# Gate and decay arithmetic of a gated-linear-attention layer, spread in 21 steps over the projections of keys, queries and values

## The chip, the cores and the metric

The kernel runs on one core of a Trainium2 chip. A core has a tensor engine for matrix products (PE, with its weight loads shown as PEld), a vector engine (DVE), a scalar engine for functions such as Exp (ACT), a general engine (POOL) and a queue engine that issues most transfers (SP). Each engine works through its own list of instructions in order and waits at an instruction until what it needs is there. The metric is the device time of one execution in microseconds (us); three runs before the change gave 1467.38 us in the median (1467.37 to 1469.64).

## The reference

One layer of a streaming encoder: a token mixer of two kinds of heads, cross-attention to 256 memory tokens, and an MLP, all on 1024 tokens of width 1024. What the change touches is the start of the mixer:

```python
proj = xn @ w_in                       # xn = rms_norm(x)
fq, fk, fv, ff, gq, gk, gv, glr, gr = split(proj)
fq = rms_norm(fq per head); fk = rms_norm(fk per head)
log_f = log_sigmoid(ff + fox_b_f)                       # 8 forget gates a token
g_log = log_sigmoid(glr @ gla_w_gate2 + gla_b_gate) / 16  # 256 decays a token
# gated linear attention, chunks of 64 tokens:
bc = cumsum(g_log over the chunk)
q_dec = gq * 64**-0.5 * exp(bc);  k_dec = gk * exp(-bc)
A = tril(q_dec @ k_dec.T);  o = A @ gv + q_dec @ state
```

The forgetting attention (called fox in the code) uses the cumulated sum of log_f as a bias on its scores.

## The kernel before, in words

All products are made of float32 operands split into two parts (hi and lo), so one tile of 128 tokens by 512 columns takes 3 x 8 matmuls of 512 columns (`gemm`, L108 to L110). The weights of 512 columns come in four transfers (`raw`, two buffers, L78); ACT makes the hi part `wh` (L97) and DVE the lo part `wl` (L98). The pool of `wh` and `wl` has nine places each, so the weights of the next projection can only be made as the last tile of the present one lets go of its own.

`mixer_inputs` runs, in this order of the program: the GLA queries and keys (`gqk`), the small columns for gates (`smallz`), the gate arithmetic, eight tiles of fox keys (`normed`, into `kd`), eight tiles of fox queries (`normed`, into `qd`), eight tiles of GLA values (`gv`, L492), then the GLA loop over eight blocks (L509 on, which begins with `ga`, L519), and the fox values (`evac_split` into `vd`).

A tile of keys or queries in `normed` goes: 24 matmuls into a PSUM bank (four banks), ACT squares it (`sq`, L141), DVE sums the squares (`ss`, L143), POOL makes the reciprocal root (`rs_v`, `rs_r`, L126 and L127), DVE scales the tile (`sq`, L304), for queries POOL multiplies by a gain (L306), PE transposes it (`tr`, L309, two PSUM banks), ACT and DVE split it (`qn`, L115 and L116), and SP writes it out.

The gate arithmetic has three rows of work: the forget gates (8 partitions, `small`, `fu`, `lf`) and two tiles of decays (128 partitions by 1024, `z` from PE at L432, then `ls`, `kdec` and `qdec` as scratch). For each: DVE min, ACT Abs and Exp, DVE add (L437 to L440), two more DVE operations (L441, L442), ACT Ln and DVE subtract (L444, L445). Then `forget` (a scan over the tokens, a split, eight small writes to `cq` and `ck`), two scans over the decays (L454), the chunk ends `La` and `Lb`, `dec`, and at L471 to L477 four Exp of the whole tile, which make `qdec` (DVE, L475) and `kdec` (POOL, L477). The first matmul that needs these two is `ga` at L519.

The order of instructions on each engine is set by a scheduler from the program's order and its own estimate of times. In the program the gate arithmetic stands wholly ahead of the keys, and L471 to L477 ahead of the queries. Behind the mixer's inputs come the fox stage (softmax blocks, with "side work" between them: half of the output projection and the keys and values of the memory, through a tile `mkv` with one buffer, written to `kTd` and `vmd`), the rest of the output projection, the cross-attention and the MLP.

Of the kernel before, what the change touches and what calls it, by code (L numbers as in the profile page):

```python
# [17 lines left out]
F32 = mybir.dt.float32  # L18
# [3 lines left out]
AF = mybir.ActivationFunctionType  # L22
ALU = mybir.AluOpType
AX = mybir.AxisListType
PSUM = bass.MemoryType.PSUM
# [5 lines left out]
P = 128  # L31
KT = D // P
NT = S // P
# [5 lines left out]
C_MIX, C_XAT, C_MEM, C_MLP, C_BG, C_FB = 0, 8, 16, 24, 32, 34  # L39
# [5 lines left out]
W_FQ, W_FK, W_FV, W_FF, W_GQ, W_GK, W_GV, W_GLR, W_GR = 0, 512, 1024, 1536, 1544, 1800, 2056, 2568, 2584  # L45


def f(ap):
    return ap.bitcast(F32)


class Layer:
# [59 lines left out]
    def evac_split(self, hi, lo, ps, scale=None):  # L112
        nc = self.nc
        if scale is None:
            nc.scalar.activation(hi, ps, AF.Copy)  # L115
            nc.vector.tensor_tensor(lo, ps, f(hi), ALU.subtract)  # L116
        else:
            nc.scalar.activation(hi, ps, AF.Identity, scale=scale)
            nc.vector.scalar_tensor_tensor(lo, ps, scale, f(hi), ALU.mult, ALU.subtract)

    def rstd(self, out, ss, inv_n, eps=EPS):

# [146 lines left out]
    def mixer_inputs(self):  # L269
        nc = self.nc  # L270
        w_in = self.w_in
        with ExitStack() as st:
# [24 lines left out]

            def normed(t, W, dst, g=None):

                ps = token_major(t, W)  # L300
                v3 = lambda ap: ap.rearrange("p (h d) -> p h d", h=8)
                qn = self.T(stp, [P, 512], F32, "sq")
                r = self.head_rstd(ps, qn, 8, self.xev[:, t:t + 1])
                nc.vector.tensor_tensor(v3(qn), v3(ps), self.bcast(r, 64), ALU.mult)  # L304
                if g is not None:
                    nc.gpsimd.tensor_tensor(v3(qn), v3(qn), g.unsqueeze(1).to_broadcast([P, 8, 64]), ALU.mult)  # L306
                tp = self.T(trp, [P, 512], F32, "tr")
                for j in range(4):
                    nc.tensor.transpose(tp[:, j * P:(j + 1) * P], qn[:, j * P:(j + 1) * P], self.ident)  # L309
                q2 = self.T(stp, [P, 2, 4, P], F32R, "qn")  # L310
                self.evac_split(q2[:, 0], q2[:, 1], tp.rearrange("p (a b) -> p a b", a=4))
                for a in range(2):
                    for i in range(2):
                        nc.sync.dma_start(dst[a::2, i, :, t * P:(t + 1) * P].rearrange("h d s -> d h s"),
                                          f(q2[64 * a:64 * a + 64, i]))

            gqk = self.mixg.rearrange("p t k s -> p (t k s)").rearrange("p (i s) -> p i s", i=4)
            with ExitStack() as s2:  # L320
# [14 lines left out]
                def factors(t):  # L335
# [23 lines left out]
                for i in range(4):  # L359
                    ps = next(gbanks)  # L360
# [3 lines left out]
                with self.tc.issue_after(x_load.ins):  # L364
                    W = self.wsplit(w_in[:, W_FK:W_FK + 512], C_MIX)
# [13 lines left out]
            for k in range(KT):  # L379
                g = self.cols[:, C_MIX + k:C_MIX + k + 1]  # L380
# [18 lines left out]
            g3 = self.T(gp, [96, 256], F32R, "g3")  # L399
# [10 lines left out]
            qdec = self.T(decp, [P, 2, 2, S], F32, "qdec")  # L410
            kdec = self.T(decp, [P, 2, S], F32, "kdec")
# [12 lines left out]

            R = slice(32, 40)
            gates = [(small[R], self.cols[R, C_FB:C_FB + 1], small[R], f(fu[R]), lf[R])]
            for ft in range(2):
                z = self.T(zps, [P, 2, 512], F32, "z")  # L430
                for h in range(2):
                    nc.tensor.matmul(z[:, h, :], g3[:, ft * P:(ft + 1) * P], s3[:, h * 512:(h + 1) * 512],  # L432
                                     start=True, stop=True)
                gates.append((z.rearrange("p a b -> p (a b)"), self.cols[:, C_BG + ft:C_BG + ft + 1], kdec[:, ft, :],
                              qdec[:, 0, ft, :], ls[:, ft, :]))
            for z, b, e, u, out in gates:
                nc.vector.tensor_scalar(out, z, b, 0.0, ALU.add, ALU.min)  # L437
                nc.scalar.activation(e, z, AF.Abs, bias=b)
                nc.scalar.activation(e, e, AF.Exp, scale=-1.0)
                nc.vector.tensor_scalar(u, e, 1.0, None, ALU.add)  # L440
                nc.vector.scalar_tensor_tensor(e, u, -1.0, e, ALU.add, ALU.subtract)  # L441
                nc.vector.tensor_tensor(out, out, e, ALU.add)  # L442
            for z, b, e, u, out in gates:
                nc.scalar.activation(u, u, AF.Ln)  # L444
                nc.vector.tensor_tensor(out, out, u, ALU.subtract)  # L445
            self.forget(lf, fu, ones)

            nc.gpsimd.memset(qdec[64:128, :, 0, :], 0.0)
            nc.gpsimd.memset(qdec[0:64, :, 1, :], 0.0)


            for ft in range(2):
                bc = kdec[:, ft, :]
                nc.vector.tensor_tensor_scan(bc, seg, ls[:, ft, :], 0.0, ALU.mult, ALU.add)  # L454
                v = bc.rearrange("p (c s) -> p c s", s=P)
                nc.vector.tensor_copy(La[:, ft, :].unsqueeze(2), v[:, :, 63:64])
                nc.vector.tensor_copy(Lb[:, ft, :].unsqueeze(2), v[:, :, 127:128])
                nc.vector.tensor_tensor(v[:, :, 0:64], v[:, :, 0:64], self.bcast(La[:, ft, :], 64), ALU.subtract)
            nc.vector.tensor_tensor(dec[:, :, 0:7], Lb[:, :, 0:7], La[:, :, 1:8], ALU.add)
            nc.scalar.activation(dec[:, :, 0:7], dec[:, :, 0:7], AF.Exp, scale=1.0 / 16)  # L460


            for t in range(NT):
                normed(t, W, self.kd)

            W = self.wsplit(w_in[:, W_FQ:W_FQ + 512], C_MIX)

            for i in range(4):
                ft = i % 2
                e = ls[:, ft, :]  # L470
                nc.scalar.activation(e, kdec[:, ft, :], AF.Exp, scale=(1.0 if i < 2 else -1.0) / 16)  # L471
                if i < 2:
                    for a in range(2):
                        r = slice(64 * a, 64 * a + 64)
                        nc.vector.scalar_tensor_tensor(qdec[r, ft, a, :], gqk[r, i, :], 0.125, e[r], ALU.mult, ALU.mult)  # L475
                else:
                    nc.gpsimd.tensor_tensor(kdec[:, ft, :], gqk[:, i, :], e, ALU.mult)  # L477

            for t in range(NT):
                normed(t, W, self.qd, self.gfox)  # L480
            gst.close()
            banks = self.two(mmp, 1, mmp, 1)

            gps = self.open(glst, "gps", 1, space=PSUM)

# [3 lines left out]
            W = self.wsplit(w_in[:, W_GV:W_GV + 512], C_MIX)  # L489
            for t in range(NT):  # L490
                ps = token_major(t, W)
                nc.scalar.activation(gv[:, t, :], ps, AF.Identity, scale=self.xr2[:, t:t + 1])  # L492


            glp = self.open(glst, "gl", 2)
# [77 lines left out]
    def forget(self, lf, ch, ones):  # L573

        nc = self.nc
        R, R0 = slice(32, 40), slice(0, 8)
        nc.gpsimd.memset(ones[R], 1.0)
        nc.vector.tensor_tensor_scan(lf[R], ones[R], lf[R], 0.0, ALU.mult, ALU.add)
        nc.scalar.activation(ch[R], lf[R], AF.Copy)
        nc.vector.tensor_tensor(lf[R], lf[R], f(ch[R]), ALU.subtract)  # L580
        nc.sync.dma_start(self.cq[:, 0, :], ones[R])
# [8 lines left out]
        nc.sync.dma_start(self.ck[:, 1, :], lf[R0])  # L590


    def fox_open(self):
# [721 lines left out]
```

## Time and profile before

| what | value |
|---|---|
| median of three runs | 1467.38 us |
| the profiled execution | 1473.37 us |
| its span from first to last instruction | 1471.6 us |
| PE busy | 1435.6 us (98%) |
| DVE, ACT, POOL busy | 934.8, 685.1, 431.7 us |
| granted PE clock, mean | 0.989 |

The profiled execution is 5.99 us longer than the median of the runs without a profile, and 1.8 us of it lie outside the span. A "waits" view lists, for one engine, the idle time in front of a line and the instruction that ended it. A "timeline" gives start, duration and instruction in order of time; the start of a matmul and its end overlap with its neighbours, so the time that one costs is read as the distance between starts. A "windows" view gives the busy time of each engine in a stretch, with the granted PE clock (1.00 is full speed).

### The profile page before, as it was taken

The page shows a single profiled execution, that of the slowest core. Times are in us where ns is not written, and L with a number is a line of the kernel's source. Part 1 is how long each engine was busy: PE and PEld are TensorE (multiplying, and loading weights), DVE is VectorE, ACT ScalarE, POOL GpSimd, SP SyncE. Part 2 cuts the span into 40 slices and gives each one's busy share as a digit, 9 for nine tenths or more (in the row PEclk, how much of TensorE's full clock was granted, in tenths as well). Part 3 has the DMA queues.
Part 4 walks back from the last instruction along what each step waited for, and adds up shares of the span by engine and source line. Part 5 has one row for each costly group of instructions (what it writes and reads, how often), then busy time and mean ns, then how long its engine had stood idle before and what let it go on. Part 6 is the DMA issues. An engine that isn't in the chain of part 4 may idle for free.

```text
span 1471.6 us, 19266 instructions
## 1 busy us (share of the span) xinstructions
PE 1435.6 (98%) x7068; PEld 1198.2 (81%) x7068; DVE 934.8 (64%) x1328; ACT 685.1 (47%) x1095; POOL 431.7 (29%) x456
## 2 busy tenths in 40 slices
PE   9999999999998999999999999999999999999998
PEld 7777888887877787888888878887888878888887
DVE  5387412427776676656654885645556958788797
ACT  4464322326776555445442254545445736334230
POOL 4146503324473311621212200000000532333454
PEclk9999999999999999999999999999999999999999
DMA  7425620268576742414375124444445846337353
GB/s 273 124 47 129 153 74 4 72 159 266 181 205 197 194 156 70 144 38 136 115 243 214 44 72 172 172 172 162 169 160 212 313 132 210 126 110 231 108 205 122
DMA packets 121166, 223.94 MB, mean 152 GB/s; under 512 B 8912, under 2 KB 54512, under 8 KB 118512
## 3 DMA queue, kind: packets, MB, share of 16 engines
q1 hardware_dynamic: 119776, 218.25, 45.9%
q10 hardware_dynamic: 1296, 4.46, 1.0%
q8 instruction: 56, 0.92, 0.3%
q14 instruction: 38, 0.31, 0.1%
HBM read 150.59 MB, written 72.09 MB: 151 GB/s over the span
## 4 chain that ended last, share of the span: by engine, by line
PE 82%; DMA 7%; DVE 4%; ACT 3%; issue 2%; POOL 1%; SPq 0%; DVEq 0%; ACTq 0%
PE mm L108 14%; PE mm L109 14%; PE mm L110 13%; PE my L109 7%; PE my L110 7%; PE my L108 7%; PE tr L109 3%; PE tr L108 3%; PE tr L110 3%; PE tr L668 2%; DMA xt<-in_x_dram 1%; DMA raw<-in_w_in_dram 1%; PE pv L675 1%; PE pv L676 1%; PE s L628 1%
## 5 line engine op out<-in xcount | busy, mean ns | idle before, releaser
L108 PE MATMUL my<-x,g 128*128 128x512 f32 x464 | 180.8, 390 | 1.5 <-ACT h L1251 1.5
L109 PE MATMUL my<-x,g 128*128 128x512 f32 x464 | 180.9, 390 | 1.3 <-DVE x L1046 1.3
L110 PE MATMUL my<-x,g 128*128 128x512 f32 x464 | 180.7, 390 | 0.0
L108 PE MATMUL mm<-wh,xh 128*128 128x512 f32 x320 | 128.7, 403 | 0.3 <-ACT wh L97 0.3
L109 PE MATMUL mm<-wl,xh 128*128 128x512 f32 x320 | 127.7, 399 | 0.0
L110 PE MATMUL mm<-wh,xl 128*128 128x512 f32 x320 | 127.4, 398 | 0.0
L1045 ACT ACTIVATE g<-s 128x1024 fp32r<-128x1024 f32 (+1 forms) x72 | 68.9, 963 | 103.9 <-PE my L110 37.6
L1046 DVE TENSOR_TENSOR g<-raw,g 128x512 fp32r<-128x512 f32 (+3 forms) x72 | 67.9, 946 | 69.2 <-ACT g L1045 69.1
L1071 POOL TENSOR_TENSOR s<-raw 128x384 f32<-128x384 f32 (+1 forms) x20 | 25.6, 1279 | 282.9 <-issue 217.0
L108 PEld LDWEIGHTS my<-x,g 128*128 128x128 f32 x464 | 87.2, 188 | 19.9 <-ACT h L1251 1.9
L109 PEld LDWEIGHTS my<-x,g 128*128 128x128 f32 x464 | 87.2, 188 | 19.6 <-DVE x L1046 1.7
L1045 ACT ACTIVATE g<-raw 128x512 fp32r<-128x512 f32 (+3 forms) x72 | 55.5, 773 | 101.8 <-DMA raw<-in_mlp_w_dram 39.9
L110 PEld LDWEIGHTS my<-x,g 128*128 128x128 f32 x464 | 87.2, 188 | 18.0
L1046 DVE TENSOR_TENSOR g<-s,g 128x1024 fp32r<-128x1024 f32 (+1 forms) x72 | 88.7, 1236 | 7.2 <-ACT g L1045 7.2
L639 POOL TENSOR_SCALAR p<-p,rrec 128x128 f32<-128x128 f32 (+3 forms) x64 | 50.6, 792 | 126.6 <-DVE rrec L638 117.0
L1213 DVE TENSOR_TENSOR x<-x 128x1024 fp32r<-128x1024 f32 (+1 forms) x64 | 77.1, 1226 | 15.7 <-ACT x L1212 15.7
L108 PE MATMUL mm<-x,g 128*128 128x512 f32 x220 | 85.9, 390 | 0.0
L110 PE MATMUL mm<-x,g 128*128 128x512 f32 x220 | 85.8, 390 | 0.0
L109 PE MATMUL mm<-x,g 128*128 128x512 f32 x220 | 85.7, 390 | 0.0
L108 PE MATMUL tr<-x,g 128*128 128x512 f32 x212 | 82.6, 389 | 0.0
L110 PE MATMUL tr<-x,g 128*128 128x512 f32 x212 | 82.6, 389 | 0.0
L109 PE MATMUL tr<-x,g 128*128 128x512 f32 x212 | 82.6, 389 | 0.0
(319 smaller groups left out, 3787.3 us busy)
## 6 DMA issues: line engine op xcount, KB each, us to landing
ud<-h SPq DMA_DIRECT2D x32, 768.0 KB
x<-ud SPq DMA_DIRECT2D x48, 512.0 KB
raw<-in_mlp_w_dram SPq DMA_DIRECT2D x20, 1024.0 KB
raw<-in_mlp_w_dram SPq DMA_DIRECT2D x16, 768.0 KB
raw<-in_w_in_dram SPq DMA_DIRECT2D x23, 512.0 KB
raw<-in_xattn_wkv_dram SPq DMA_DIRECT2D x16, 512.0 KB
od<-o SPq DMA_DIRECT2D x32, 256.0 KB
ud<-h SPq DMA_DIRECT2D x32, 256.0 KB
```

The costliest lines, as they stand in the source:

```text
L108: mm(ps, lh[k], rh[k], start=start and k == 0, stop=False, **kw)
L109: mm(ps, lh[k], rl[k], start=False, stop=False, **kw)
L110: mm(ps, ll[k], rh[k], start=False, stop=stop and k == n - 1, **kw)
L628: nc.tensor.matmul(ps[:, c], qa[:, ts], ka[:, c], start=True, stop=False)
L639: nc.gpsimd.tensor_scalar(p[:, 0:n], p[:, 0:n], rr, 1.0, ALU.mult, ALU.mult)
L668: nc.tensor.transpose(o, pp[i][:, kb * P:(kb + 1) * P], self.ident)
L675: nc.tensor.matmul(pv, va[:, kb, :], th[:, js], start=kb == 0, stop=False)
L676: nc.tensor.matmul(pv, va[:, kb, :], tl[:, js], start=False, stop=kb == nb - 1)
L1045: self.nc.scalar.activation(hi, src, AF.Copy)
L1046: self.nc.vector.tensor_tensor(lo, src, f(hi), ALU.subtract)
L1071: eng.tensor_tensor(s[:, 0], raw[:, 3], raw[:, 2], ALU.add)
L1213: nc.vector.tensor_tensor(lo, f(lo), f(hi), ALU.subtract)
```

## The change

The gate and decay arithmetic becomes a generator, `decays()`, that stops at 21 places. The function `step(*ends)` runs it to the next stop and puts everything it makes on an engine behind the instruction of that engine that is given in `ends`. A step is taken behind the eviction (`evac_split`: one instruction of ACT and one of DVE) of key tiles 0 to 5, of query tiles 0 to 5, and behind the ACT eviction of each of the eight tiles of `gv`; there only the ACT instructions of the step are tied, and POOL's are tied nowhere. What is left runs after the last `gv` tile. The two tiles of decays now go ahead of the forget gates; all three Abs and Exp come before the three Ln; the forget gates' scan and their writes come behind the Ln; and the PSUM pools of `z` and of the fourth bank are held until the end of the `gv` tiles. No arithmetic is added or left out.

```diff
     def evac_split(self, hi, lo, ps, scale=None):
...
+            a = nc.scalar.activation(hi, ps, AF.Copy)
+            v = nc.vector.tensor_tensor(lo, ps, f(hi), ALU.subtract)
...
+        return a.ins, v.ins
...
+            def decays():
+                gates = []
+                for ft in (0, 1, None):
...
                     nc.vector.tensor_scalar(out, z, b, 0.0, ALU.add, ALU.min)
                     nc.scalar.activation(e, z, AF.Abs, bias=b)
                     nc.scalar.activation(e, e, AF.Exp, scale=-1.0)
                     nc.vector.tensor_scalar(u, e, 1.0, None, ALU.add)
+                    yield
                     nc.vector.scalar_tensor_tensor(e, u, -1.0, e, ALU.add, ALU.subtract)
                     nc.vector.tensor_tensor(out, out, e, ALU.add)
+                    gates.append((u, out))
+                    yield
+                for u, out in gates:
+                    nc.scalar.activation(u, u, AF.Ln)
+                    nc.vector.tensor_tensor(out, out, u, ALU.subtract)
+                    yield
+                yield from self.forget(lf, fu, ones)
...
+            beside = decays()
+
+            def step(*ends):
+                with ExitStack() as behind:
+                    for ins in ends:
+                        behind.enter_context(self.tc.issue_after(ins))
+                    next(beside, None)
+
+            for cols, dst, g in ((W_FK, self.kd, None), (W_FQ, self.qd, self.gfox)):
+                if cols == W_FQ:
+                    W = self.wsplit(w_in[:, cols:cols + 512], C_MIX)
+                for t in range(NT):
+                    ends = normed(t, W, dst, g)
+                    if t < 6:
+                        step(*ends)
...
             for t in range(NT):
                 ps = token_major(t, W)
-                nc.scalar.activation(gv[:, t, :], ps, AF.Identity, scale=self.xr2[:, t:t + 1])
+                step(nc.scalar.activation(gv[:, t, :], ps, AF.Identity, scale=self.xr2[:, t:t + 1]).ins)
+            for _ in beside:
+                pass
+            gst.close()
```

The order that results on the engines differs at these places. The numbers behind the names tell tiles apart; they are not the same in both kernels.

On DVE, in the middle of the key tiles, before the change (`kdec`, `qdec`, `ls`, `La`, `Lb` are the decays; `sq`, `ss`, `qn` belong to the key tiles):

```order
L116 TENSOR_TENSOR qn_863<-tr_858,qn_863 128x512
L143 TENSOR_REDUCE ss_183_943<-sq_941 128x8
L454 SCALAR_TENSOR_TENSOR kdec_664<-seg_655,ls_675 128x1024
L304 TENSOR_TENSOR sq_895<-mm_870,rs_r_899 128x512
L441 SCALAR_TENSOR_TENSOR kdec_664<-qdec_663,kdec_664 128x1024
L456 COPY La_669<-kdec_664 128x8
L457 COPY Lb_670<-kdec_664 128x8
L304 TENSOR_TENSOR sq_941<-mm_916,rs_r_945 128x512
```

And the same tiles of keys (the fourth and fifth that are made) after it:

```order
L449 SCALAR_TENSOR_TENSOR kdec_664<-qdec_663,kdec_664 128x1024
L144 TENSOR_REDUCE ss_176_857<-sq_855 128x8
L450 TENSOR_TENSOR ls_675<-ls_675,kdec_664 128x1024
L305 TENSOR_TENSOR sq_855<-mm_830,rs_r_859 128x512
L116 TENSOR_TENSOR qn_816<-tr_811,qn_816 128x512
L444 TENSOR_SCALAR ls_675<-z_823,cols_74 128x1024
L144 TENSOR_REDUCE ss_183_905<-sq_903 128x8
L447 TENSOR_SCALAR qdec_663<-kdec_664 128x1024
L305 TENSOR_TENSOR sq_903<-mm_878,rs_r_907 128x512
```

The scan (L454) has left the key tiles; it stands at query tiles 3 and 7 now. Ahead of the scaling of the fourth tile stand two decay operations of the first tile of decays, and ahead of that of the fifth two of the second, one on each side of a sum (`ss`).

On ACT, from the sixth tile of `gv` on, before the change (`wh` are the weights of the next projection, of which the first is made earlier):

```order
L492 ACTIVATE gv_1535<-mm_1706,xr_19_83 128x512
L492 ACTIVATE gv_1535<-mm_1732,xr_19_83 128x512
L97 ACTIVATE wh_1803<-raw_1797,cols_74 128x512
L97 ACTIVATE wh_1809<-raw_1807,cols_74 128x512
L97 ACTIVATE wh_1813<-raw_1807,cols_74 128x512
L97 ACTIVATE wh_1819<-raw_1817,cols_74 128x512
L97 ACTIVATE wh_1823<-raw_1817,cols_74 128x512
L492 ACTIVATE gv_1535<-mm_1758,xr_19_83 128x512
L97 ACTIVATE wh_1829<-raw_1827,cols_74 128x512
```

And after it (L477 are the Exp that were at L471):

```order
L510 ACTIVATE gv_1510<-mm_1693,xr_19_83 128x512
L477 ACTIVATE ls_675<-kdec_664 128x1024 x2
L510 ACTIVATE gv_1510<-mm_1721,xr_19_83 128x512
L97 ACTIVATE wh_1803<-raw_1797,cols_74 128x512
L97 ACTIVATE wh_1809<-raw_1807,cols_74 128x512
L97 ACTIVATE wh_1813<-raw_1807,cols_74 128x512
L97 ACTIVATE wh_1819<-raw_1817,cols_74 128x512
L97 ACTIVATE wh_1823<-raw_1817,cols_74 128x512
L510 ACTIVATE gv_1510<-mm_1748,xr_19_83 128x512
L477 ACTIVATE ls_675<-kdec_664 128x1024
L97 ACTIVATE wh_1829<-raw_1827,cols_74 128x512
```

The last Exp stands behind the last `gv` tile, and POOL makes the last half of `kdec` from it. On PE the first `ga` has moved too: before, its first matmul stood behind 4 matmuls of the next projection (`mm` of `gr`, counted from the last one of `gv`), now it stands behind 43 of them.

On SP, in the fox stage, around the third write of memory keys (`kTd`), before the change (`qa`, `ka`, `qb`, `kb` are the next head's operands):

```order
L608 DMA qa_4450<-qd_57 128x1024
L609 DMA ka_4452<-kd_58 64x1024
L610 DMA ka_4452<-kd_58 64x1024
L611 DMA qb_4451<-qd_57 64x1024
L612 DMA kb_4453<-kd_58 64x1024
L753 DMA kTd_62<-mkv_4046 256x4x128
L613 DMA qb_4451<-cq_60 4x1024
```

And after it:

```order
L634 DMA qa_4450<-qd_57 128x1024
L635 DMA ka_4452<-kd_58 64x1024
L779 DMA kTd_62<-mkv_4046 256x4x128
L636 DMA ka_4452<-kd_58 64x1024
L637 DMA qb_4451<-qd_57 64x1024
L638 DMA kb_4453<-kd_58 64x1024
L639 DMA qb_4451<-cq_60 4x1024
```

The scheduler has put this write ahead of three loads of 256 KB. Rearrangements of this kind go through the whole fox stage on all five engines, although no line of it was changed.

More of the change, by code (lines that the diff above doesn't have):

```diff
@@ L114, in evac_split @@
         if scale is None:
-            nc.scalar.activation(hi, ps, AF.Copy)
-            nc.vector.tensor_tensor(lo, ps, f(hi), ALU.subtract)
-        else:
-            nc.scalar.activation(hi, ps, AF.Identity, scale=scale)
-            nc.vector.scalar_tensor_tensor(lo, ps, scale, f(hi), ALU.mult, ALU.subtract)
+            a = nc.scalar.activation(hi, ps, AF.Copy)
+            v = nc.vector.tensor_tensor(lo, ps, f(hi), ALU.subtract)
+        else:
+            a = nc.scalar.activation(hi, ps, AF.Identity, scale=scale)
+            v = nc.vector.scalar_tensor_tensor(lo, ps, scale, f(hi), ALU.mult, ALU.subtract)
+        return a.ins, v.ins
     def rstd(self, out, ss, inv_n, eps=EPS):
@@ L310, in normed @@
                 q2 = self.T(stp, [P, 2, 4, P], F32R, "qn")
-                self.evac_split(q2[:, 0], q2[:, 1], tp.rearrange("p (a b) -> p a b", a=4))
+                ends = self.evac_split(q2[:, 0], q2[:, 1], tp.rearrange("p (a b) -> p a b", a=4))
                 for a in range(2):
@@ L315, in normed @@
                                           f(q2[64 * a:64 * a + 64, i]))
+                return ends
             gqk = self.mixg.rearrange("p t k s -> p (t k s)").rearrange("p (i s) -> p i s", i=4)
@@ L427, in mixer_inputs @@
             R = slice(32, 40)
[L428 to L484, printed above, removed]
+            def decays():
+                gates = []
+                for ft in (0, 1, None):
+                    if ft is None:
+                        z, b, e, u, out = small[R], self.cols[R, C_FB:C_FB + 1], small[R], f(fu[R]), lf[R]
+                    else:
+                        z = self.T(zps, [P, 2, 512], F32, "z")
+                        for h in range(2):
+                            nc.tensor.matmul(z[:, h, :], g3[:, ft * P:(ft + 1) * P], s3[:, h * 512:(h + 1) * 512],
+                                             start=True, stop=True)
+                        z, b, e, u, out = (z.rearrange("p a b -> p (a b)"), self.cols[:, C_BG + ft:C_BG + ft + 1],
+                                           kdec[:, ft, :], qdec[:, 0, ft, :], ls[:, ft, :])
+                    nc.vector.tensor_scalar(out, z, b, 0.0, ALU.add, ALU.min)
+                    nc.scalar.activation(e, z, AF.Abs, bias=b)
+                    nc.scalar.activation(e, e, AF.Exp, scale=-1.0)
+                    nc.vector.tensor_scalar(u, e, 1.0, None, ALU.add)
+                    yield
+                    nc.vector.scalar_tensor_tensor(e, u, -1.0, e, ALU.add, ALU.subtract)
+                    nc.vector.tensor_tensor(out, out, e, ALU.add)
+                    gates.append((u, out))
[5 more added lines that the diff above has]
+                yield from self.forget(lf, fu, ones)
+                nc.gpsimd.memset(qdec[64:128, :, 0, :], 0.0)
+                nc.gpsimd.memset(qdec[0:64, :, 1, :], 0.0)
+                for ft in range(2):
+                    bc = kdec[:, ft, :]
+                    nc.vector.tensor_tensor_scan(bc, seg, ls[:, ft, :], 0.0, ALU.mult, ALU.add)
+                    yield
+                    v = bc.rearrange("p (c s) -> p c s", s=P)
+                    nc.vector.tensor_copy(La[:, ft, :].unsqueeze(2), v[:, :, 63:64])
+                    nc.vector.tensor_copy(Lb[:, ft, :].unsqueeze(2), v[:, :, 127:128])
+                    nc.vector.tensor_tensor(v[:, :, 0:64], v[:, :, 0:64], self.bcast(La[:, ft, :], 64), ALU.subtract)
+                    yield
+                nc.vector.tensor_tensor(dec[:, :, 0:7], Lb[:, :, 0:7], La[:, :, 1:8], ALU.add)
+                nc.scalar.activation(dec[:, :, 0:7], dec[:, :, 0:7], AF.Exp, scale=1.0 / 16)
+                for i in range(4):
+                    ft = i % 2
+                    e = ls[:, ft, :]
+                    nc.scalar.activation(e, kdec[:, ft, :], AF.Exp, scale=(1.0 if i < 2 else -1.0) / 16)
+                    if i < 2:
+                        for a in range(2):
+                            r = slice(64 * a, 64 * a + 64)
+                            nc.vector.scalar_tensor_tensor(qdec[r, ft, a, :], gqk[r, i, :], 0.125, e[r], ALU.mult, ALU.mult)
+                            yield
+                    else:
+                        nc.gpsimd.tensor_tensor(kdec[:, ft, :], gqk[:, i, :], e, ALU.mult)
+                        yield
@@ L491, in mixer_inputs @@
                 ps = token_major(t, W)
-                nc.scalar.activation(gv[:, t, :], ps, AF.Identity, scale=self.xr2[:, t:t + 1])
+                step(nc.scalar.activation(gv[:, t, :], ps, AF.Identity, scale=self.xr2[:, t:t + 1]).ins)
+            for _ in beside:
+                pass
+            gst.close()
+            banks = self.two(mmp, 1, mmp, 1)
+            gps = self.open(glst, "gps", 1, space=PSUM)
             glp = self.open(glst, "gl", 2)
@@ L580, in forget @@
         nc.vector.tensor_tensor(lf[R], lf[R], f(ch[R]), ALU.subtract)
+        yield
         nc.sync.dma_start(self.cq[:, 0, :], ones[R])
@@ L590, in forget @@
         nc.sync.dma_start(self.ck[:, 1, :], lf[R0])
+        yield
     def fox_open(self):
```

## Prediction

> **What bounds the kernel now.** I read the chain of work that ended last, then PE's waits by line, then PE's timeline around the waits of the changed stage, and at last the other engines there.
>
> ```profile
> PE 82%; DMA 7%; DVE 4%; ACT 3%; issue 2%; POOL 1%; SPq 0%; DVEq 0%; ACTq 0%
> ```
>
> PE carries 82% of the chain. Work on DVE, ACT or POOL therefore costs time only where PE waits for it, and moving it pays only what such waits cost. PE's longest waits and one short one:
>
> ```profile
> PE tr L309 <- DVE sq L304: 5.2, 2, 3.0
> PE mm L108 <- DVE mkv L119: 4.0, 2, 3.0
> PE tr L668 <- DVE mkv L116: 2.9, 1, 2.9
> ...
> PE mm L108 <- ACT wh L97: 0.3, 1, 0.3
> ```
>
> The columns are total us, count and longest. The first row lies in the changed stage: transposes of key tiles wait for DVE's scaling. The `mkv` rows are of the fox stage, far behind. The windows (length, then busy time of PE, PEld, DVE, ACT and POOL, each with a count, then granted PE clock, DMA share and GB/s) show where DVE is full:
>
> ```profile
> 80.00:100.00 20.00, 20.00 (x96) 16.53 (x95) 17.71 (x18) 14.65 (x16) 8.15 (x4) 1.00 0.25 45
> 100.00:120.00 20.00, 16.43 (x68) 12.63 (x66) 19.38 (x25) 13.40 (x18) 12.86 (x8) 0.91 0.52 109
> 120.00:140.00 20.00, 18.05 (x79) 14.90 (x80) 16.05 (x23) 8.37 (x13) 13.85 (x12) 0.91 0.63 154
> ...
> 340.00:360.00 20.00, 18.15 (x100) 14.88 (x98) 13.58 (x27) 10.40 (x24) 9.05 (x12) 0.91 1.02 298
> ```
>
> From 100 to 120 us DVE works 19.38 of 20 us, PE 16.43, and the granted clock is 0.91 there and in the next window, against 1.00 before.
>
> **The change part by part.** *Term 1, the two waits.*
>
> ```profile
> 108.04 0.63 PE L309 MATMUL tr<-ident,sq 128*128 128x128 f32 x4 [2.99 <-DVE sq L304]
> 108.42 0.66 PE L108 MATMUL mm<-wh,xh 128*128 128x512 f32 x1
> ...
> 112.15 0.39 PE L108 MATMUL mm<-wh,xh 128*128 128x512 f32 x1
> ...
> 113.53 0.39 PE L108 MATMUL mm<-wh,xh 128*128 128x512 f32 x1
> ...
> 119.24 0.49 PE L108 MATMUL mm<-wh,xh 128*128 128x512 f32 x1 [0.31 <-ACT wh L97]
> ...
> 121.95 0.86 PE L309 MATMUL tr<-ident,sq 128*128 128x128 f32 x4 [2.22 <-DVE sq L304]
> 122.46 0.77 PE L108 MATMUL mm<-wh,xh 128*128 128x512 f32 x1
> ...
> 125.85 0.39 PE L110 MATMUL mm<-wh,xl 128*128 128x512 f32 x1
> ```
>
> The waits are 2.99 + 2.22 + 0.31 = 5.52 us, and what follows them is slow. From 108.42 to 112.15 nine matmuls start in 3.73 us; from 112.15 to 113.53 six take 1.38, so 0.23 each (0.228 over longer stretches), and nine should take 2.05: 1.68 lost. From 122.46 to 125.85 eight take 3.39 instead of 1.82: 1.57 lost. That is 3.25 us of slow clock, and the two belong together: 5.52 + 3.25 = **8.8 us**.
>
> A wait of 2.22 us is already followed by the slow spacing. The Trainium skill ("TensorE: Matmul & The Clock Gate", "Why this matters for your kernels") asks for no PE gap over about 3 us, as if a shorter one left the clock alone. The trace disagrees, so the measurement decides; by that rule the slow stretches would come from something else and stay, and the gain would be 5.5 us.
>
> Why the two scalings were late stands on DVE, with POOL's input in the last row:
>
> ```profile
> 105.03 2.27 DVE L454 TENSOR_TENSOR_SCAN kdec<-seg,ls 128x1024 f32<-128x1024 bf16 x1
> 107.23 0.66 DVE L304 TENSOR_TENSOR sq<-mm,rs_r 128x512 f32<-128x512 f32 x1
> ...
> 117.55 2.27 DVE L454 TENSOR_TENSOR_SCAN kdec<-seg,ls 128x1024 f32<-128x1024 bf16 x1
> 119.86 1.22 DVE L475 SCALAR_TENSOR_TENSOR qdec<-mixg,ls 64x1024 f32<-64x1024 f32 x1
> 121.11 0.69 DVE L304 TENSOR_TENSOR sq<-mm,rs_r 128x512 f32<-128x512 f32 x1
> 102.28 2.53 POOL L127 TENSOR_TENSOR rs_r<-rs_v,mhalf 128x8 f32<-128x8 f32 x1
> ```
>
> `rs_r` was ready at 104.81, but a scan of 2.27 us stood ahead of the scaling; at the second wait a scan and a `qdec` product, 3.5 us together. Both leave the key tiles. What is late next is reckoned per tile. PE takes 24 x 0.228 = 5.5 us for one. DVE's own part and the chain from the last matmul to the scaling:
>
> ```profile
> 75.27 0.60 ACT L141 ACTIVATE sq<-mm 128x512 f32<-128x512 f32 x1 [9.74 <-PE mm L110]
> 75.90 0.69 DVE L143 TENSOR_REDUCE ss<-sq 128x8 f32<-128x512 f32 x1 [3.74 <-ACT sq L141]
> 76.70 0.28 POOL L126 TENSOR_SCALAR rs_v<-ss,xev 128x8 f32<-128x8 f32 x1 [24.47 <-DVE ss L143]
> 77.06 1.65 POOL L127 TENSOR_TENSOR rs_r<-rs_v,mhalf 128x8 f32<-128x8 f32 x1
> ...
> 85.71 1.28 DVE L437 TENSOR_SCALAR ls<-z,cols 128x1024 f32<-128x1024 f32 x1
> 92.82 0.70 DVE L440 TENSOR_SCALAR qdec<-kdec 128x1024 f32<-128x1024 f32 x1
> 93.56 1.23 DVE L441 SCALAR_TENSOR_TENSOR kdec<-qdec,kdec 128x1024 f32<-128x1024 f32 x1
> ```
>
> The chain is 0.60 + 0.69 + 0.28 + 1.65 + 0.69 = 3.9 us. DVE spends three operations of 0.69 on a tile, 2.1 us; a step adds 1.28 + 0.70 = 2.0 or, with L442 taken like L441, 2.5. So DVE is busy 4.1 to 4.6 of 5.5 us, and nothing accumulates over the key tiles. The new order puts the transposes of a tile 35 matmuls (8.0 us) or more behind its last one. Going through the new lists with these durations, I find each scaled tile at least 2.5 us before PE comes to it; the least margins are at query tiles 5 and 7 and at the last key tile. So I take no new wait. Bounds: nothing, or one wait of the kind just shown in its smaller form, 2.22 + 1.7 = 3.9 us.
>
> *The scans among the queries.* One stands ahead of the scaling of query tile 3, one at the last. With the small copies and the subtraction this is some 3.3 us beside the tile's 2.1, nearly the whole 5.5 us of a tile, and POOL is between (`rs_v`, `rs_r`, then the gain). One pair of rows speaks against it:
>
> ```profile
> 90.51 2.28 DVE L578 TENSOR_TENSOR_SCAN lf<-ones,lf 8x1024 f32<-8x1024 f32 x1
> 90.58 2.29 POOL L126 TENSOR_SCALAR rs_v<-ss,xev 128x8 f32<-128x8 f32 x1 [3.39 <-DVE ss L143]
> ```
>
> An `rs_v` that takes 0.28 us alone took 2.29 beside a scan, so a scan can delay POOL's part of the next tile by 2.0 us. The Trainium skill ("SBUF — State Buffer", "Who interferes with whom") says that a DVE instruction with two SBUF inputs blocks a GpSimd instruction that reads SBUF until it is done; the trace agrees. 2.0 us is less than the margin of 2.5, so I cost it at nothing; if the margin is used up, it is rival B.
>
> *The last steps, at the `gv` tiles.* The first `ga` needs the last half of `kdec`, which is now made after the last `gv`.
>
> ```profile
> 115.31 1.07 ACT L471 ACTIVATE ls<-kdec 128x1024 f32<-128x1024 f32 x1
> 122.31 2.38 POOL L477 TENSOR_TENSOR kdec<-mixg,ls 128x1024 f32<-128x1024 f32 x1 [3.85 <-ACT ls L471]
> ...
> 207.70 0.69 ACT L492 ACTIVATE gv<-mm,xr 128x512 f32<-128x512 f32 x1 [4.75 <-PE mm L110]
> ...
> 214.92 0.67 ACT L492 ACTIVATE gv<-mm,xr 128x512 f32<-128x512 f32 x1
> ```
>
> The seventh tile is evicted at 207.70, so PE ends the eighth about 213.1, and its eviction, behind weights on ACT, begins at 214.92. Add 0.67, the Exp (1.07) and the POOL product (2.38): 219.0, some 6 us behind PE. In the new order 43 matmuls, 9.8 us, stand between. So `ga` has 3.7 us to spare: nothing. The bounds are nothing and, if the weights' loads land 5 us later, 1.3 us of wait and 1.7 of clock.
>
> *Behind that.* PE is busy all the time from 140 to 240 us:
>
> ```profile
> 140.00:240.00 100.00, 100.00 (x490) 83.42 (x488) 30.88 (x48) 29.38 (x47) 32.28 (x30) 1.00 0.37 88
> ```
>
> So the 8.8 us travel on as an earlier start. In the fox stage the scheduler has reshuffled all queues without a cause that I can price. The one place with a price is the single buffer of `mkv`:
>
> ```profile
> 450.41 1.12 PE L668 MATMUL tr<-ident,p 128*128 128x128 f32 x4 [2.92 <-DVE mkv L116]
> 450.00:460.00 10.00, 9.59 (x49) 8.23 (x50) 7.66 (x16) 7.13 (x17) 2.74 (x4) 0.66 0.36 108
> 490.00:500.00 10.00, 9.04 (x47) 7.88 (x48) 7.30 (x15) 5.88 (x13) 4.36 (x6) 0.83 0.53 166
> ```
>
> The waits there are 4.0 + 2.9 = 6.9 us, and the clock of 0.66 and 0.83 over 10 us costs 3.4 + 1.7 = 5.1: 12.0 in all. The new order puts `kTd`'s write ahead of three loads of 256 KB, which should free `mkv` sooner, but gives PE less work between two uses of it. I take 0, with bounds of -12.0 (all of it goes) and +14.1 (three more waits of 3.0 with 1.7 of clock).
>
> **Sum.** The profiled execution took 1473.37 us (span 1471.6); minus 8.8 that is 1464.6. It lies 5.99 above the median of the runs, so against these the forecast is 1467.4 - 8.8 = **1458.6 us**.
>
> **The rivals.**
>
> *B, a new wait among the queries* (0.12): a scan keeps POOL or DVE, a transpose waits about 2.0 us, and 1.7 us of clock follow: 3.7 given back, 1462.3. For it speaks the pair of rows above, against it the margin.
>
> *C, slower: more `mkv` waits* (0.10). Each further wait for the one buffer costs 3.0 + 1.7 = 4.7 us. From 8.8 us on it outweighs the gain, which is two more waits; three give 1467.4 - 8.8 + 14.1 = 1472.7. For it speaks that three such waits exist already and that the order is new there, against it the earlier write.
>
> *D, a late `kdec`* (0.03): the 3.0 us at the first `ga`, 1461.6.
>
> *E, the gain is swallowed behind* (0.10). The window from 340 to 360 has a DMA share of 1.02 and 298 GB/s, and PE idles 1.85 us in it. If transfers set the start of the fox stage, an earlier PE only waits longer: 1467.4. Against it: the loads are issued as buffers come free, so they start earlier too.
>
> *F, the `mkv` waits largely go* (0.03): about 1450.
>
> *G, the slow stretches are not due to the waits* (0.02): 1467.4 - 5.5 = 1461.9; the trace speaks against it, since both begin right behind one.
>
> The forecast itself, within 4 us (1454.6 to 1462.6), has 0.60.
>
> **How the numbers follow.** 0.2%, or 2.9 us, is about what a measurement of this kernel can tell. Faster, under 1464.5: most of the forecast, B, D, F and G, with 0.06 taken off for mixtures of these with a further `mkv` wait, 0.74. The same: E, the mildest of C and most of the mixtures, 0.17. Slower, over 1470.3: C with three waits, 0.09. The range goes from 1452.5, about half of the `mkv` bound below the forecast, to 1468.0, which holds B, D, E and G and two further `mkv` waits (1468.0); F and C proper stay outside.
>
> **What would show it right or wrong.** Right: no wait of a key transpose for DVE over 0.5 us, the clock at 1.00 from 100 to 140 us, and the first `gv` matmul some 9 us earlier. B would be a wait of a query transpose for POOL or DVE; D a wait of `ga` for POOL; E a start of the fox stage that isn't earlier; C and F other totals in the two `mkv` rows. Wrong in its first term would be waits on the keys that stay although the scans are gone.

## The result, and the profile after

The changed kernel took 1458.51 us in the median of four runs (1456.5 to 1462.09), the kernel before 1468.04 (1467.37 to 1469.64): a ratio of 0.9932, with a 95% interval from 0.9915 to 0.9949. Two further comparisons gave 0.9921 (0.9904 to 0.9937) and 0.9929 (0.9903 to 0.9955). The forecast was 1458.6. The profiled execution took 1456.50 us, its span 1454.8: 2.0 us below the median and the fastest of the four runs, while the profile of before lay 5.3 us above its median. Differences between these two profiles are therefore larger than those between the runs.

PE's waits by line in the profile after (total us, count, longest):

```profile
PE s L654 <- ACT p L662: 3.2, 4, 1.3
PE mm L108 <- ACT sh L828: 2.4, 1, 2.4
PE pv L701 <- ACT pth L115: 2.1, 1, 2.1
...
PE mm L108 <- DVE mkv L119: 1.3, 1, 1.3
...
PE mm L108 <- DVE sq L305: 1.0, 2, 0.7
PE mm L109 <- DVE wl L98: 0.8, 1, 0.8
```

The waits of key transposes for DVE, 5.2 us before, have gone. But there are two lines that were not there: matmuls that wait for `sq` and for `wl`. And of the 6.9 us at `mkv` only 1.3 are left, in a part of the program that the change doesn't touch. The windows of the stage:

```profile
100.00:120.00 20.00, 20.00 (x95) 16.54 (x94) 16.90 (x23) 11.18 (x17) 8.05 (x6) 1.00 0.71 170
120.00:140.00 20.00, 20.00 (x96) 16.54 (x95) 10.44 (x15) 6.54 (x9) 12.09 (x10) 1.00 0.57 121
140.00:160.00 20.00, 18.52 (x87) 14.67 (x85) 16.01 (x18) 7.82 (x12) 12.28 (x10) 1.00 0.41 85
160.00:180.00 20.00, 19.58 (x89) 15.37 (x90) 14.35 (x21) 7.10 (x12) 9.95 (x7) 1.00 0.66 164
```

PE is full at clock 1.00 where it had lost 5.5 us, and idles 1.9 us between 140 and 180, where it had been full. The timeline of PE, DVE and POOL shows that new place:

```profile
151.52 2.98 DVE L602 TENSOR_TENSOR_SCAN lf<-ones,lf 8x1024 f32<-8x1024 f32 x1
155.14 1.40 DVE L98 SCALAR_TENSOR_TENSOR wl<-raw,cols,wh 128x512 fp32r<-128x512 f32 x2
156.57 1.22 DVE L604 TENSOR_TENSOR lf<-lf,fu 8x1024 f32<-8x1024 f32 x1
157.82 0.75 DVE L98 SCALAR_TENSOR_TENSOR wl<-raw,cols,wh 128x512 fp32r<-128x512 f32 x1
159.32 0.69 DVE L305 TENSOR_TENSOR sq<-mm,rs_r 128x512 f32<-128x512 f32 x1 [0.75 <-POOL rs_r L128]
155.33 1.27 POOL L127 TENSOR_SCALAR rs_v<-ss,xev 128x8 f32<-128x8 f32 x1 [2.96 <-DVE ss L144]
156.68 2.60 POOL L128 TENSOR_TENSOR rs_r<-rs_v,mhalf 128x8 f32<-128x8 f32 x1
158.63 0.50 PE L109 MATMUL mm<-wl,xh 128*128 128x512 f32 x1 [0.84 <-DVE wl L98]
160.07 0.50 PE L108 MATMUL mm<-wh,xh 128*128 128x512 f32 x1 [0.70 <-DVE sq L305]
```

The forget gates' scan, now a step behind the fourth query tile, and the subtraction at 156.57 stand ahead of the weights `wl` of `gv`. The scan also stands ahead of the sum `ss` of the fifth query tile, for which POOL sits idle 2.96 us before its `rs_v`; `rs_v` and `rs_r` are then slow beside DVE (1.27 and 2.60 us, against 0.28 and 1.65 where DVE was idle in the profile before). So the scaling comes late, and a matmul waits for the PSUM bank that it frees.

To see where the time went, the span is cut at three marks that both kernels have: the first matmul of `z`, the eviction of the seventh `gv` tile, which ACT makes as soon as PE ends the tile, and the last `pv` of the fox stage. The windows of the two stretches between them, first the kernel before and then the changed one:

```profile
84.18:207.70 123.52, 118.00 (x535) 96.71 (x534) 70.24 (x91) 49.78 (x70) 58.67 (x46) 0.97 0.47 104
207.70:577.10 369.40, 353.02 (x2038) 298.26 (x2037) 217.86 (x404) 197.63 (x402) 135.70 (x166) 0.97 0.52 151
```

```profile
80.83:198.27 117.44, 115.54 (x535) 94.11 (x534) 75.15 (x93) 47.81 (x68) 49.85 (x40) 1.00 0.49 109
198.27:562.30 364.03, 350.03 (x2037) 293.23 (x2036) 216.12 (x404) 197.36 (x403) 145.62 (x172) 0.99 0.53 153
```

The first stretch ("the stage") is 6.1 us shorter, the second ("the fox stretch") 5.4, and 3.4 us lie ahead of `z`, where nothing was changed. The fox stretch begins with the GLA loop; up to the first matmul `s` of the softmax, 110 to 114 us, PE has no idle time and the clock is 1.00 in all thirteen profiles, so its waits all lie behind. The experiments ask which of these is the change's doing.

### The profile page after: what moved, and what is told of

Same layout as the page of the kernel before. It is cut to its first block, busy times and chain, and to the rows that moved or that the text cites. A ratio compares the mean times of both kernels' runs of the same rounds, so it can differ in the third digit from the quotient of the medians.

```text
span 1454.8 us, 19244 instructions
## 1 busy us (share of the span) xinstructions
PE 1428.4 (98%) x7068; PEld 1189.1 (82%) x7068; DVE 936.0 (64%) x1328; ACT 679.1 (47%) x1091; POOL 434.9 (30%) x456
## 4 chain that ended last, share of the span: by engine, by line
PE 81%; DMA 9%; DVE 4%; ACT 3%; issue 2%; POOL 1%; SPq 0%; ACTq 0%; DVEq 0%; POOLq 0%
PE mm L108 14%; PE mm L109 13%; PE mm L110 13%; PE my L109 7%; PE my L110 7%; PE my L108 7%; PE tr L109 3%; PE tr L108 3%; PE tr L110 3%; DMA raw<-in_xattn_wkv_dram 1%; PE tr L694 1%; DMA xt<-in_x_dram 1%; DMA raw<-in_w_in_dram 1%; DMA kTd<-mkv 1%; PE pv L701 1%
## 5 line engine op out<-in xcount | busy, mean ns | idle before, releaser
L110 PEld LDWEIGHTS my<-x,g 128*128 128x128 f32 x464 | 87.1, 188 | 18.1
```

The costliest lines, as they stand in the source:

```text
L110: mm(ps, ll[k], rh[k], start=False, stop=stop and k == n - 1, **kw)
```

## The experiments

All kernels were read at the same marks. "Slow" is what a granted clock under 1.00 takes away, summed over forty equal windows of the stretch (length times one minus clock); idle is the length less PE's busy time. Us throughout. The two are not terms of a sum: from the first row to the third they fall by 9.1 us in the fox stretch, and the stretch falls by 5.4.

| kernel | stage (idle, slow) | fox stretch (idle, slow) | ratio to before, 95% |
|---|---|---|---|
| before | 123.5 (5.5, 3.4) | 369.4 (16.4, 10.2) | 1 |
| before, again | 125.1 (6.1, 5.1) | 368.3 (16.3, 8.6) | 1 |
| changed | 117.4 (1.9, 0) | 364.0 (14.0, 3.5) | 0.9932 (0.9915 to 0.9949) |
| changed, again | 117.5 (1.9, 0) | 362.3 (12.9, 3.4) | 0.9921 (0.9904 to 0.9937) |
| changed, third | 118.0 (1.6, 1.7) | 364.4 (13.3, 5.1) | 0.9929 (0.9903 to 0.9955) |
| no query steps | 114.2 (0, 0) | 372.6 (21.0, 5.0) | 0.9946 (0.9933 to 0.9959) |
| three at keys | 124.4 (6.2, 1.7) | 368.5 (18.2, 5.2) | 1.0013 (1.0004 to 1.0022) |
| scans at queries | 117.8 (2.7, 0) | 372.1 (19.4, 6.9) | 0.9976 (0.9962 to 0.9990) |
| before, two `mkv` | 123.5 (5.5, 3.4) | 370.0 (16.7, 8.5) | 1.0012 (1.0001 to 1.0023) |
| changed, two `mkv` | 117.5 (1.9, 0) | 373.2 (18.1, 8.5) | 0.9995 (0.9979 to 1.0011) |
| no query steps, two `mkv` | 114.6 (0, 0) | 367.8 (16.0, 5.2) | 0.9936 (0.9917 to 0.9955) |
| two query steps | 116.4 (0.9, 0) | 364.2 (13.0, 5.2) | 0.9938 (0.9916 to 0.9960) |
| rest at values | 114.3 (0, 0) | 363.7 (13.8, 3.5) | 0.9920 (0.9900 to 0.9940) |

**Both kernels again.** No edit.

> The kernel before, profiled a second time. Two stretches are read: from the first matmul of z (84.2 us in the first profile, 80.8 in the profile after the change, although nothing ahead of it was changed) to the eviction of the seventh tile of gv (207.70 and 198.27), so 123.5 us before and 117.5 after; and from there to the end of the span, 1263.9 and 1256.5. Theory 1 (the gain is the two waits of key transposes and the slow clock behind them, less 1.85 us of new short waits): the first stretch is again 123 to 124 us, with the same two waits on DVE sq; the 3.4 us ahead of z are a difference between executions, so z may lie anywhere from 80.5 to 84.5. Theory 2 (a good part of the gain comes from the rearranged fox stage): the second stretch is again 1262 to 1265. If theory 1 is the whole of it, the second stretch is within 2 us of 1256.5.

> The changed kernel, timed in five rounds and profiled a second time. Theory 1: from z to the seventh eviction of gv 117 to 118 us, no wait of a key transpose, the three short waits on wl and sq between 155 and 176 us again; ratio to the kernel before 0.992 to 0.996. Theory 2: from the seventh eviction of gv to the end of the span 1255 to 1258, clearly below that of the kernel before.

The stage repeats to 0.1 us in the changed kernel (117.46) and is 1.6 us longer in the kernel before, where the second wait was 3.03 us instead of 2.22. The fox stretch repeats to 1.8 us, so its gain of 5 to 6 us is no chance of one execution: theory 2 holds beside theory 1. The start is chance: `z` lay at 81.75 and 84.17 in these, the other way round than in the first pair.

**No steps at the queries.** A step at all eight key tiles, two at each `gv` tile:

```diff
-                    if t < 6:
+                    if cols == W_FK:
                         step(*ends)
...
+                step(end)
+                step(end)
```

> The changed kernel with a step behind each of the eight key tiles, none at the queries, and two behind each tile of gv. The scans then stand at the second and third query tile and the forget gates' scan beside the last queries, none of them beside the weights wl of gv. Theory 1: the three short waits of 1.85 us go, nothing new of over 1 us comes, from z to the seventh eviction 115.5 to 116 us; time 1 to 2 us under the changed kernel, if the fox stage, which is ordered anew, stays as it is. Rival (a scan that stands straight ahead of a scaling makes PE wait wherever it stands): waits of 2 to 3 us and a slow clock at the second and third query tile, from z to the seventh eviction 120 us or more, time 2 us or more above the changed kernel.

The stage was as theory 1 had it and better: 114.25 us without one wait, 3.2 us under the changed kernel. So the new waits among the queries cost 3.2 us, more than their idle time of 1.9: the wait of 0.84 holds the next start 1.23 us behind the last, where 0.23 is usual. But the fox stretch was 372.6 us, and the time was above the changed kernel, by 3.5 us in the medians. (This profile is the slowest of the variant's five runs, 5.0 us above their median, so its fox stretch may be longer than usual.) The waits of its fox stage, by line:

```profile
PE s L656 <- ACT p L664: 5.6, 4, 3.3
PE mm L108 <- DVE mkv L119: 4.2, 1, 4.2
PE tr L696 <- POOL p L667: 2.2, 5, 0.8
```

Its order there differs from that of both kernels; but for a few rows it is that of the next two variants too.

**Three steps at each key tile.** The edit has all key tiles; the 21 steps are used up at the seventh.

```diff
-                    if t < 6:
-                        step(*ends)
+                    if cols == W_FK:
+                        for _ in range(3):
+                            step(*ends)
```

> The changed kernel with three steps behind each of the first six key tiles and none at the queries, so that the scans, the forget gates and the weights of the queries meet on DVE among the key tiles again, though the work is still tied step by step. Theory 1 (it is the load on DVE beside the key tiles that counts): waits of PE on DVE sq come back, 4 to 8 us in all, with a granted clock under 1.00 behind those of 2 us or more; from z to the seventh eviction 122 to 128 us, time that of the kernel before within 4 us. Rival (tying the steps behind evictions is enough): from z to the seventh eviction at most 119 us, time that of the changed kernel within 2 us.

The rival falls: tied, but crowded at the keys, the work makes PE wait as before (one of its eleven runs took 2895 us and is not in the ratio; the others took 1469.8 to 1474.6). The stage took 124.4 us. The waits on the scaled tile, 2.8 us, are less than the 4 to 8 expected; waits on the weights come beside them:

```profile
PE tr L310 <- DVE sq L305: 2.8, 2, 2.4
PE mm L109 <- DVE wl L98: 2.4, 3, 1.2
```

**The scans and what follows them moved.** The gates, their Ln and the forget gates' scan stay untied at the keys; the two scans over the decays and the rest are tied to the queries:

```diff
             beside = decays()
+            for _ in range(11):
+                next(beside)
...
-                    if t < 6:
+                    if cols == W_FQ:
                         step(*ends)
```

> One part of the change alone: the gates, their Ln and the forget gates' scan stand at the keys without ties, as in the kernel before; only the two scans over the decays and what follows them are tied, one step to each query tile, the rest to the gv tiles. Theory 1 (the two scans straight ahead of a scaling are the cause): the two waits of key transposes go although the gates still crowd the key tiles; waits on the keys under 1 us in all; from z (or, as z stands later here, from the first key transpose) to the seventh eviction of gv 115 to 119 us against 123.5 to 125 before. Rival (the load of all the gate work on DVE): waits of key transposes of 2 us and more stay. From the seventh eviction to the end 1255 to 1267 by any theory, since the fox stage is ordered anew.

Half right. The stage fell to 117.8 us, the waits of key transposes to 2.6 us, but not under 1:

```profile
103.50 0.63 PE L310 MATMUL tr<-ident,sq 128*128 128x128 f32 x4 [0.81 <-DVE sq L305]
114.94 0.63 PE L310 MATMUL tr<-ident,sq 128*128 128x128 f32 x4 [1.78 <-DVE sq L305]
```

The two scans, with all that follows them (the `qdec` products too, of which one stood ahead of the second late scaling before), are half of the cause: of 5.2 to 6.0 us of such waits 2.6 are left. The first of these comes behind gate operations on DVE. Ahead of the second stands POOL:

```profile
109.18 1.80 POOL L460 MEMSET qdec<- 64x2048 f32 x1 [1.92 <-DVE ls L455]
111.08 1.27 POOL L127 TENSOR_SCALAR rs_v<-ss,xev 128x8 f32<-128x8 f32 x1
114.11 0.69 DVE L305 TENSOR_TENSOR sq<-mm,rs_r 128x512 f32<-128x512 f32 x1 [1.21 <-POOL rs_r L128]
```

Its `rs_v` stands behind a clearing of `qdec`, a part of the decay arithmetic that is tied nowhere, and is slow itself; DVE is idle 1.21 us until `rs_r` is there. The clock stayed at 1.00 behind both waits and no slow time was left; behind the wait of 1.78 us that may be luck, since other waits of that length were followed by a slow clock (last section).

**Two buffers for `mkv`,** in three kernels:

```diff
-                kv = self.T(mp, [P, 2, 512], F32R, "mkv")
+                kv = self.T(mp, [P, 2, 512], F32R, "mkv", bufs=2)
```

> The kernel before with two buffers for mkv. Theory 2a (what the new order gained behind the gv tiles, 5.7 us from the seventh eviction of gv to the last pv of the fox stage, 363 against 369 us, is fewer and shorter waits for the one buffer): the waits on mkv go, 6.9 us with their clock, and the stretch takes 357 to 364 us; time 5 to 12 us under the kernel before. Rival 2b (the fox stage is bound by other chains, the softmax of ACT, POOL and DVE, and mkv is only where they show): other waits take their place and the stretch stays at 366 or more.

> The changed kernel with two buffers for mkv. Theory 2a: only one wait of 1.3 us on mkv is left there, so little changes: the stretch from the seventh eviction to the last pv takes 361 to 364 us, and the time is within 2 us of the changed kernel; against the kernel before with two buffers only the stage of keys, queries and values is left as a gain, 6 to 7.5 us. Rival 2b: the stretch differs by more than 3 us either way, as the order is a new draw.

> The variant without steps at the queries, with two buffers for mkv. It had the shortest stage of keys, queries and values (114.25 us from z to the seventh eviction, no wait at all) and lost 10 us behind it, 372.7 us to the last pv, with waits of 4.16 on mkv and 3.34 of s for ACT. Theory 2a: the stretch falls to 361 to 366 us and the time to 1451 to 1457, under both kernels. Rival 2b: the wait of s for ACT and others stay or grow, the stretch stays over 368, time 1459 to 1463.

Theory 2a falls. With a second buffer the kernel before was no better in the stretch (370.0), and the changed kernel lost 10 us of it (373.2) and with them its whole gain, although its stage was the same to 0.1 us. This edit alters nothing ahead of the fox stage; what it alters there, beside the buffer, is the order. Nor do the waits of that name go. The first row below is of the kernel before with two buffers; in the kernel with one, the wait of 3.00 us for `mkv` at 490.96 had nothing to do with the buffer either: the second row is DVE's work straight ahead of that `mkv` (490.17), for whose `sh` ACT had been held up 3.15 us by a load of weights. PE waits there for the PSUM bank that is evicted into `mkv`.

```profile
447.94 0.50 PE L108 MATMUL mm<-wh,sh 128*128 128x512 f32 x1 [2.98 <-DVE mkv L119]
```

```profile
487.91 2.34 DVE L803 TENSOR_TENSOR sl<-mixf,sh 128x512 fp32r<-128x512 f32 x2
```

In the changed kernel with two buffers PE waits for ACT in the softmax instead:

```profile
PE pv L701 <- ACT pth L115: 4.3, 2, 3.2
PE s L654 <- ACT p L662: 4.0, 4, 1.8
```

Only the third got nearer to what theory 2a expected: 367.8 after 372.6, between its range and that of the rival; its time, 1460.2 us, is in the rival's range, and a wait of 2.4 us on `mkv` stayed.

**The same fox order with other stages.** Two spreads of the steps were taken for which the scheduler falls into the changed kernel's own order in the fox stage (with two query steps the same rows on PE, DVE, ACT and SP; with the rest at the values the same rows on all engines from 12 us behind the first `s` on):

```diff
 # two query steps: 8 at the keys, 2 at the queries, 2 at each of the first two gv tiles
-                    if t < 6:
+                    for _ in range(1 if cols == W_FK else int(t < 2)):
...
+                for _ in range(1 + int(t < 2)):
+                    step(end)
 # rest at values: 6 at the keys, none at the queries, 2 at each gv tile
-                    if t < 6:
+                    for _ in range(int(t < 6) if cols == W_FK else 0):
...
+                for _ in range(2):
+                    step(end)
```

> The changed kernel with a step behind each of the eight key tiles, behind the first two query tiles, and two behind each of the first two gv tiles, one behind the rest. The forget gates' scan now stands four query tiles ahead of the weights wl of gv; and on PE, DVE, ACT and SP the fox stage has instruction for instruction the order of the changed kernel, not that of the variant without steps at the queries. Theory 3 (what happens behind the gv tiles is set by which of a few orders the scheduler falls into, not by when the stage begins): the stage of keys, queries and values takes 114 to 115 us from z to the seventh eviction, without a wait over 0.5 us, as in that variant, and the stretch from there to the last pv 361.5 to 364.5 us as in the changed kernel; time 2 to 4 us under the changed kernel and 5 to 8 under the variant without steps at the queries. Rival 3b (the stretch depends on when it begins, against the transfers): it takes 366 or more although its order is the same, and the time is that of the changed kernel or above.

> The changed kernel with a step behind each of the first six key tiles, none at the queries and two behind each gv tile, so that both scans over the decays, the forget gates' scan and all four Exp fall beside the gv tiles. The fox stage has again the order of the changed kernel on DVE and ACT, and nearly on PE. Theory 3: z to the seventh eviction 114 to 115 us, the stretch behind it 361.5 to 365, time as with two query steps within 2 us. Rival D of the prediction (a late kdec at the first ga, since all is made at the last moment): a wait of PE for kdec, qdec or the scans of 2 us or more, time 4 us or more above the variant with two query steps.

> The changed kernel a third time, for comparison within this call. Theory 3: from z to the seventh eviction 117.4 to 117.5 us, from there to the last pv 362 to 364.5 us; the ratio to the kernel before 0.991 to 0.9945. If its stretch behind the gv tiles comes out at 366 or more, the gain of 5.7 us there was chance of two executions.

Theory 3 holds for the fox stretch: 364.2 and 363.7 us, with 364.4 for the changed kernel measured beside them. Five profiles with this order lie between 362.3 and 364.4, though they begin it anywhere from 194.3 to 201.6 us; the eight with other orders between 367.8 and 373.2. An order doesn't fix the time to the microsecond, though: the three variants that share a third one (no query steps, three at keys, scans at queries) took 372.6, 368.5 and 372.1, and the last two have the same order on all engines from mark to mark. The stage of the changed kernel's third execution took 118.0 us, not the 117.4 to 117.5 expected, with one slow stretch behind waits of 0.86 and 0.71 us. The windows of the kernel with the rest at the values:

```profile
80.03:194.29 114.26, 114.26 (x535) 94.48 (x534) 72.51 (x93) 46.48 (x68) 45.48 (x39) 1.00 0.50 112
194.29:558.00 363.71, 349.91 (x2037) 293.17 (x2036) 220.95 (x404) 198.51 (x404) 144.15 (x172) 0.99 0.54 153
```

PE has no idle time in the stage, and the late `kdec` of rival D cost nothing. With two query steps two short waits of 0.54 and 0.28 us stayed, and the stage took 116.4 us, not 114 to 115. In time neither is apart from the changed kernel: 1457.19 and 1458.80 against 1458.42 us beside them, and all intervals overlap. The 3 us that the better stage shows in the profile are not established in the runs.

## Why the prediction was right, and where it was not

**Term 1** was right in mechanism and size. In the kernel before the stage loses 5.5 us of idle time and 3.4 of slow clock, 8.9 together against 8.8 forecast, and in the changed kernel no key transpose waits and the clock is 1.00. That the scans, with one `qdec` product, caused it alone is too much: with them and all that follows them moved, half of those waits stayed. Where these waits are gone the clock of the stage is 1.00, but for one execution with two short waits of another kind; rival G falls with that.

**"So I take no new wait"** is the step that failed. The reckoning of margins followed the transposes alone, and these do have time. It left out two other consumers of the same DVE queue: the matmul that needs the PSUM bank freed by the scaling, and the weights `wl` of `gv`. There lie the new waits, 1.9 us, which cost 3.2 of the stage. The prediction names two scans among the queries; the waits come behind a third, that of the forget gates. It is near rival B's mechanism: the scan keeps DVE, and so holds up the sum that POOL's `rs_v` needs, but a matmul waits and not a transpose, with a slow clock behind it in only one of the three profiles. So the stage gave 6.1 us in the first pair of profiles and 7.6 in the second, not 8.8. The sign that the prediction names, `gv` some 9 us earlier, came in part by chance: the seventh eviction is 9.4 us earlier in the first pair, of which 3.4 lie ahead of `z`, and 5.2 in the second.

**"I take 0" for the fox stage** was off by 5 to 6 us in these profiles, inside its bounds. The two errors have opposite signs, and the forecast is as near as it is for that reason too. That is luck: the prediction gave the fox stage nothing. The price that the prediction put there, waits for the one `mkv` buffer, was the wrong handle: 3.00 of its 6.9 us were no wait for the buffer, and a second buffer didn't shorten the stretch. What moves is how many waits of all kinds come and how many are followed by a slow clock. That the order makes it is shown as far as thirteen profiles go (the changed kernel with two buffers loses about 10 us with the same stage; other stages with the same order keep 364; the five with that order lie below all eight others); which rows of the order make it is not, and stays open.

**Rivals.** C did not come with this change, but the size that it allowed for is real: from 362 to 373 us, the draw of the order is worth more than the whole gain of the stage. E is refuted: the fox stretch begins earlier by all that the stage gained, and is not longer for it. (Its first `s`, counted from `z`, comes only 2.1 and 3.6 us earlier, because the new order puts 4.0 us more of PE's work ahead of it, without idle time.) D did not come. F came in its waits and not in its time: of 6.9 us at `mkv` 1.3 are left, but other waits came or grew (3.2 us for `p`, 2.4 for `sh`, 2.1 for `pth`), and the stretch gave 5 to 6 us, not 12.

One thing doesn't add up. From `z` to the end the profiles of before take 1387.4 and 1388.1 us, those of the changed kernel 1374.0, 1373.2 and 1376.7, 11 to 15 us less, while the runs differ by 9.5 to 10.9 in the median. The two profiled executions of before lay 2.4 and 5.3 us above the medians of their comparisons, the three of the changed kernel between 2 below and 1 above; five profiles don't say why.

## What to carry to other kernels

When work is moved between tiles, follow every consumer of the queue that it enters: the bank that a scaling frees and the weights of the next stage count as much as the next matmul in the chain. Where a scheduler orders everything behind the edit anew, treat the later stages as a draw: measure how much that draw is worth (here up to 10 us of 365), and compare variants that fall into the same order before crediting the edit. Breaking a long stretch of vector work into steps pays where it keeps PE's waits short, since the long ones cost their slow clock on top.

## What the runs showed of the hardware

**Slow clock behind a wait comes in one size and is partly chance.** In the first 700 us of the thirteen profiles, the clock in the 4 us behind a PE wait was below 1.00 for all 22 waits from 2.38 us up, for 24 of 34 between 1.49 and 2.33, and for four between 1.1 and 1.49, each with another wait within 5 us ahead. Two pairs of waits under 1 us were followed by it too (0.83 and 0.90, 0.86 and 0.71). The slow time of each stretch in the table comes in multiples of 1.7 us, within rounding. The same wait at the same place, in two executions of the kernel before, with its window (PE's clock is the third number from the end):

```profile
567.99 0.30 PE L668 MATMUL tr<-ident,p 128*128 128x128 f32 x1 [1.55 <-DVE ptl L116]
567.99:571.99 4.00, 4.00 (x24) 3.92 (x25) 2.13 (x5) 2.05 (x6) 1.25 (x2) 0.67 0.02 4
```

```profile
567.26 0.83 PE L668 MATMUL tr<-ident,p 128*128 128x128 f32 x5 [1.55 <-DVE ptl L116]
567.26:571.26 4.00, 4.00 (x35) 3.92 (x36) 2.66 (x6) 3.08 (x8) 1.25 (x2) 1.00 0.01 4
```

In one it is followed by 24 matmuls in 4 us, in the other by 35. This goes against the rule that the prediction set beside the row, of the Trainium skill ("TensorE: Matmul & The Clock Gate", "Why this matters for your kernels"): waits of about half its 3 us can already slow the clock. Why some do and some don't was not tested.

**DVE is held up by POOL as POOL is by DVE.** In the changed kernel the scans that begin while POOL multiplies take longer, 3.10 us here instead of 2.27:

```profile
167.72 1.29 POOL L307 TENSOR_TENSOR sq<-sq,gfox 128x512 f32<-128x512 f32 x1 [0.90 <-DVE sq L305]
168.06 3.10 DVE L464 TENSOR_TENSOR_SCAN kdec<-seg,ls 128x1024 f32<-128x1024 bf16 x1
```

POOL ends at 169.01; the scan, counted back 2.27 us from its end at 171.16, would start at 168.89, 0.12 us before. The thirteen profiles have 39 scans. The 16 that begin while this multiplication runs take 2.78 to 3.10 us, and counted back each would start 0.12 to 0.13 us before it ends; the other 23 take 2.27 to 2.29, also where POOL clears a tile or makes an `rs_r`. So a scan is held until this multiplication is nearly done.
